# Products of weights and values in a differential attention: three passes of split operands in place of one native float32 matmul

## Chip, cores and metric

The kernel runs on 1 core of one Trainium2 chip. The metric is the device time of one execution in microseconds (us). The kernel before took 2629.19 us as the median of 3 runs (2627.92 to 2631.38).

## What is computed

One layer of a streaming-encoder trunk on 1024 positions of width 1024, all in float32. One input projection feeds three branches (an mLSTM, a differential attention, a retention); their outputs are gated, merged, projected, and a gated feed-forward follows. The change lies in the differential attention: 8 heads, each with two sets of scores (64 wide) and values 128 wide.

```python
def diff_attention(q, k, v, lam):
    ...
    for blk in range(S // Q_BLOCK):            # Q_BLOCK = 128, S = 1024
        q0 = blk * Q_BLOCK
        kend = q0 + Q_BLOCK
        ...
        s = jnp.einsum('bqhcd,bkhcd->bhcqk', qb, kb)
        ...
        s = jnp.where(allowed, s + bias[None, :, None], -jnp.inf)
        p = jax.nn.softmax(s, axis=-1)
        a = p[:, :, 0] - lam * p[:, :, 1]
        outs.append(jnp.einsum('bhqk,bkhe->bqhe', a, vb))
    ...
hd = (rmsnorm(hd, diff_subln[l]) * (1.0 - lam_init)).reshape(B, S, DIFF_W)
```

## The kernel before

Nearly every matmul of the kernel works on split operands: a float32 value is kept as a high part (a copy in the reduced type float32r) and a low part (the rest, also float32r). `split_sbuf` makes both, with a copy on ScalarE (L105) and a subtraction on VectorE (L106). `mm3` multiplies two split operands in three passes into one PSUM bank: high by high (L111), high by low (L112), low by high (L113). The projections, the merges of the branches, the output projection and the feed-forward are made of such passes with 512 moving columns.

The differential attention (`diff_core`) walks through 64 units, 8 heads by 8 query blocks of 128, the longest block first. A unit has up to 8 key blocks (qb + 1 of them). Its steps:

- `scores`: for both score sets, one or two PSUM buffers of scores from split q and k (L837), then the distance bias and the row maximum on VectorE (L839), then the exponential on ScalarE (L844).
- `weights`: the two exponentials are combined with the ratio of their sums (VectorE L850, L854, GpSimd L851, L853).
- `turn`: each 128x128 block of weights is transposed on TensorE (L864) into PSUM, in groups of up to four blocks, and each group is copied to SBUF (L866): the first group by ScalarE, the second by VectorE.
- `values`: one native float32 matmul for each key block (L874), with the transposed weights as the loaded operand and 128 columns of the values as the moving one. Then ScalarE takes the sum of squares (L214), GpSimd makes the factor (L220, L221), ScalarE applies it (L880).
- `finish`, one unit later: the result is transposed (L890), scaled (L891), and stored for every four units.

While unit n is turned, the scores of unit n + 2 and the weights of unit n + 1 are made. The q, k and v of the next head are loaded in the units with five and four key blocks (`diff_load`, `diff_load_v`, on the SP queue). Between the units' steps a generator hands out the merge products of the other two branches as filler for TensorE (`weave`, at a fixed rate); those left over run after the attention. The order of the instructions on each engine is made by the Tile scheduler from the program; each engine then works through its own list in that order.

Buffers: tiles of 4 KB a partition come from one pool of 32 (`big`), those of 2 KB from one of 14 (`half_tile`), and there are two sets of four PSUM banks: the value products and the merges take one, the scores and all transposes the other.

Of the kernel before, what the change touches and what calls it, by code (L numbers as in the profile page):

```python
# [9 lines left out]
F32R = mybir.dt.float32r  # L10
# [5 lines left out]
P = 128  # L16
D = 1024
S = 1024
NT = S // P
# [21 lines left out]
def trunk(ctx: ExitStack, tc: tile.TileContext, x, norm_gains, w_in, mlstm_conv, mlstm_gate_bias,  # L41
          diff_lambda, diff_subln, w_mlstm_out, w_diff_out, w_ret_out, w_out, w_ffn_in, w_ffn_out,
          c_ident, c_dist, c_tri, c_ret, c_retcol, c_reset, out):
    nc = tc.nc
# [11 lines left out]
    def nm(s):  # L56
        counter[0] += 1
        return f"{s}_{counter[0]}"

    def big(shape, dtype=F32, name="t"):  # L60
        return pool.tile(shape, dtype, tag="T", bufs=N_T, name=nm(name))

    def small(shape, tag, dtype=F32, bufs=2):
        return pool.tile(shape, dtype, tag=tag, bufs=bufs, name=nm(tag))

    def psum(dense=False):

        return psp.tile([P, HALF], F32, tag="d" if dense else "m", bufs=N_D if dense else 8 - N_D, name=nm("ps"))
# [20 lines left out]
    dv_dram = dram.tile([S, D], F32, name="dv_dram")  # L89
# [6 lines left out]
    def half_tile(shape=(P, HALF), dtype=F32):  # L96
        return pool.tile(list(shape), dtype, tag="s2k", bufs=N_H, name=nm("s2k"))
# [6 lines left out]
    def split_sbuf(hi, lo, src):  # L104
        nc.scalar.copy(hi, src)  # L105
        nc.vector.tensor_sub(lo, src, hi.bitcast(F32))  # L106

    def mm3(ps, lhs, rhs, start, stop, more=False):

        (lh, ll), (rh, rl) = lhs, rhs  # L110
        nc.tensor.matmul(ps, lh, rh, start=start, stop=False, skip_group_check=more)  # L111
        nc.tensor.matmul(ps, lh, rl, start=False, stop=False, skip_group_check=more)  # L112
        nc.tensor.matmul(ps, ll, rh, start=False, stop=stop, skip_group_check=more)  # L113
# [96 lines left out]
    def square_sum(src, n, tag, junk=None):  # L210
        if junk is None:
            junk = small([P, n], "junk", BF16 if n > HALF else F32, bufs=1)
        ss = small([P, 1], tag + "s", bufs=4)
        nc.scalar.activation(junk, src, AF.Square, accum_out=ss)  # L214
        return ss

    def factor(dst, ss, scale, extra):

        t = small([P, 1], "fv", bufs=4)
        nc.gpsimd.tensor_scalar(t, ss, scale, extra, op0=ALU.mult, op1=ALU.add)  # L220
        nc.gpsimd.tensor_tensor(dst, t, expo[:, 0:1], op=ALU.pow)  # L221
# [451 lines left out]
    def cols_at(t, a, b):  # L673
        return t[0][:, a:b], t[1][:, a:b]
# [133 lines left out]
            nc.sync.dma_start(d["q", sh][64 * i:64 * i + 64].bitcast(F32), q)  # L808

    def diff_load_v(hd, d):  # L810
        d["v"] = big([P, NT, P], name="dv")
        nc.sync.dma_start(d["v"], dv_dram[:, hd * P:(hd + 1) * P].rearrange("(t p) e -> p t e", p=P))

    diff_qk = [{} for _ in range(DH)]

    def half_cols(c):
        return slice((c % 4) * P, (c % 4 + 1) * P)

    def diff_core():
# [36 lines left out]
        def turn(u):  # L856
            qb = u["qb"]
            u["at"] = []
            for g in range((qb + 4) // 4):
                n = min(4, qb + 1 - g * 4)  # L860
                ps = psum()
                for i in range(n):
                    kb = g * 4 + i
                    nc.tensor.transpose(ps[:, i * P:(i + 1) * P], u["sb"][0][:, kb * P:(kb + 1) * P], ident)  # L864
                at = half_tile()
                (nc.scalar.copy if g == 0 else nc.vector.tensor_copy)(at[:, :n * P], ps[:, :n * P])  # L866
                u["at"].append(at)

        def values(u):
            hd, qb = u["hd"], u["qb"]  # L870
            v = diff_qk[hd]["v"]
            o_ps = psum(True)
            for kb in range(qb + 1):
                nc.tensor.matmul(o_ps[:, :P], u["at"][kb // 4][:, half_cols(kb)], v[:, kb, :],  # L874
                                 start=kb == 0, stop=kb == qb)
            ss = square_sum(o_ps[:, :P], P, "d")
            fac = small([P, 1], "dfac", bufs=4)
            factor(fac, ss, 1.0 / P, u["eps"])
            hn = u["hn"] = small([P, HD], "hk", bufs=2)
            nc.scalar.activation(hn[:, :P], o_ps[:, :P], AF.Copy, scale=fac)  # L880
# [20 lines left out]
        for n, u in enumerate(units):  # L901
            hd, qb = u["hd"], u["qb"]
# [446 lines left out]
    def head(dst, cols, kinds, hd):  # L1349
        for i, (c, evac) in enumerate(zip(cols, kinds)):  # L1350
            c += hd * HD
            yield of((c, c + P), evac(lambda j, i=i: dst[hd][:, 2 * i + j, :], hd))

    units = []
    for hd in range(MH):
        q, k, o, v = head(m_dram, (C_MQ, C_MK, C_MO, C_MV),
                          (lambda dst, hd: convolved(dst, 2 * hd), lambda dst, hd: convolved(dst, 8 + 2 * hd),
                           lambda dst, hd: stored(dst, AF.Sigmoid), lambda dst, hd: stored(dst)), hd)
# [88 lines left out]
    ps = psum()  # L1447
# [92 lines left out]
```

## Time and profile before

| what | value |
|---|---|
| median of 3 runs | 2629.19 us (2627.92 to 2631.38) |
| the profiled execution | 2628.78 us, of which 2627.0 us from the first to the last instruction (its span) |
| mean granted TensorE clock | 0.992 |
| TensorE (PE) busy | 2520.3 us, 96% of the span |
| VectorE (DVE), ScalarE (ACT), GpSimd (POOL) busy | 1650.2, 1245.9, 331.8 us |
| chain that ended last | 73% PE, 12% issue, 5% DVE, 4% ACT |
| the differential attention | from about 1347 to 1747 us of the span |

Times in rows are in us from the start of the span unless marked ns. A matmul's record is longer than its share of the engine, because matmuls are pipelined: what one costs is read from start to start. A row of the timeline gives start, length and, after the operation, how many instructions were merged in it (x14).

### The profile page before, as it was taken

What the parts mean: (1) busy time and instruction counts of PE and PEld (TensorE: products, weight loads), DVE (VectorE), ACT (ScalarE), POOL (GpSimd) and SP (SyncE); (2) the same over time, 40 slices, a digit from 0 to 9 for tenths busy, and PEclk for the clock granted to TensorE, in tenths of its full rate; (3) what the DMA queues carried; (4) which work ended last, traced back from release to release, by engine and by line L of the source; (5) the groups of instructions that cost most, each with busy time, mean ns of one, the idle gap of its engine ahead of it and who ended that gap; (6) DMA issues with size and microseconds to landing.
All of it is one profiled execution on the core that took longest, in us unless ns stands there. A gap on an engine that the chain in (4) does not pass through costs nothing.

```text
span 2627.0 us, 35171 instructions
## 1 busy us (share of the span) xinstructions
PE 2520.3 (96%) x12061; PEld 2058.6 (78%) x12061; DVE 1650.2 (63%) x3164; ACT 1245.9 (47%) x2562; POOL 331.8 (13%) x657
## 2 busy tenths in 40 slices
PE   6989999999999999999999988999989999999997
PEld 5868887888888888888878776778877888888885
DVE  7767777666656666555556665653468655656756
ACT  6554554444444444444446555542365333334444
POOL 0001111000000000000003223332121110110000
PEclk9999999999999999999999999999999999999999
DMA  4344345454445545444467566745443333327342
GB/s 127 95 125 137 115 132 153 136 150 123 127 139 161 169 145 150 137 134 121 138 193 178 140 184 157 189 157 188 144 137 112 101 104 97 105 97 288 113 143 78
DMA packets 402078, 368.93 MB, mean 140 GB/s; under 512 B 18957, under 2 KB 302046, under 8 KB 401898
## 3 DMA queue, kind: packets, MB, share of 16 engines
q1 hardware_dynamic: 399424, 364.45, 46.3%
q10 hardware_dynamic: 2474, 2.22, 0.3%
q8 instruction: 95, 1.56, 0.3%
q14 instruction: 85, 0.70, 0.1%
HBM read 249.92 MB, written 116.69 MB: 140 GB/s over the span
## 4 chain that ended last, share of the span: by engine, by line
PE 73%; issue 12%; DVE 5%; ACT 4%; POOL 3%; DMA 3%; SPq 1%; ACTq 0%; DVEq 0%; POOLq 0%
PE ps L112 22%; PE ps L113 22%; PE ps L111 22%; PE ps L874 2%; PE ps L837 1%; DMA s2k<-branch 1%; ACT sb L844 1%; POOL dfac L221 1%; PE ps L690 1%; PE ps L649 1%; POOL fv L220 1%; DVE sb L839 1%; POOL xr L208 1%; DMA ws<-in_w_in_dram 1%; DVE wl L106 0%
## 5 line engine op out<-in xcount | busy, mean ns | idle before, releaser
L105 ACT CAST wh<-ws 128x512 fp32r<-128x512 f32 (+1 forms) x622 | 385.1, 623 | 708.5 <-PE ps L112 514.1
L106 DVE TENSOR_TENSOR wl<-ws,wh 128x512 fp32r<-128x512 f32 (+1 forms) x622 | 449.8, 726 | 255.7 <-ACT wh L105 245.5
L315 DVE TENSOR_TENSOR ws<-ws,ws 128x512 f32<-128x512 f32 x234 | 160.8, 689 | 105.7 <-DMA ws<-in_w_in_dram 60.5
L111 PE MATMUL ps<-bh,wh 128*128 128x512 f32 x384 | 155.5, 405 | 1.6 <-ACT bh L105 1.6
L112 PE MATMUL ps<-bl,wh 128*128 128x512 f32 x384 | 152.5, 397 | 0.2 <-DVE bl L106 0.2
L113 PE MATMUL ps<-bh,wl 128*128 128x512 f32 x384 | 152.1, 396 | 0.0
L328 ACT COPY s2k<-ps 128x512 f32<-128x512 f32 x234 | 135.8, 581 | 11.2 <-PE ps L113 11.0
L111 PE MATMUL ps<-S2h,wh 128*128 128x512 f32 x312 | 125.7, 404 | 4.9 <-ACT s2k L328 4.9
L111 PE MATMUL ps<-A11h,wh 128*128 128x512 f32 x312 | 126.3, 405 | 2.7 <-ACT A11h L272 2.7
L112 PE MATMUL ps<-S1l,wh 128*128 128x512 f32 x312 | 123.5, 396 | 2.7 <-DVE S1l L106 2.7
L111 PE MATMUL ps<-S3h,wh 128*128 128x512 f32 x312 | 125.2, 401 | 0.9 <-ACT s2k L328 0.9
L111 PE MATMUL ps<-S1h,wh 128*128 128x512 f32 x312 | 124.2, 401 | 1.8 <-ACT S1h L105 1.7
L111 PE MATMUL ps<-A22h,wh 128*128 128x512 f32 x312 | 124.9, 400 | 0.8 <-DVE s2k L454 0.6
L112 PE MATMUL ps<-wl,wh 128*128 128x512 f32 x308 | 120.5, 392 | 4.8 <-DVE wl L106 4.8
L111 PE MATMUL ps<-S4h,wh 128*128 128x512 f32 x312 | 124.8, 400 | 0.0
L111 PE MATMUL ps<-A12h,wh 128*128 128x512 f32 x312 | 124.7, 400 | 0.0
L112 PE MATMUL ps<-S2l,wh 128*128 128x512 f32 x312 | 124.5, 400 | 0.0
L112 PE MATMUL ps<-A11l,wh 128*128 128x512 f32 x312 | 124.3, 398 | 0.1
L112 PE MATMUL ps<-A12l,wh 128*128 128x512 f32 x312 | 123.8, 397 | 0.5 <-DVE A12l L280 0.5
L113 PE MATMUL ps<-S2h,wl 128*128 128x512 f32 x312 | 124.1, 398 | 0.0
L113 PE MATMUL ps<-A11h,wl 128*128 128x512 f32 x312 | 124.0, 398 | 0.0
L113 PE MATMUL ps<-A12h,wl 128*128 128x512 f32 x312 | 123.9, 397 | 0.0
(301 smaller groups left out, 6434.1 us busy)
## 6 DMA issues: line engine op xcount, KB each, us to landing
ws<-in_w_in_dram SPq DMA_DIRECT2D x112, 512.0 KB, 4.5
ws<-in_w_ffn_in_dram SPq DMA_DIRECT2D x44, 512.0 KB, 4.3
m_dram<-s2k SPq DMA_DIRECT2D x64, 256.0 KB, 2.0
ch<-m_dram SPq DMA_DIRECT2D x32, 512.0 KB, 5.3
r_dram<-s2k SPq DMA_DIRECT2D x64, 256.0 KB, 2.3
ch<-r_dram SPq DMA_DIRECT2D x32, 512.0 KB, 4.7
qk_dram<-s2k SPq DMA_DIRECT2D x64, 256.0 KB, 2.7
dk<-qk_dram SPq DMA_DIRECT2D x64, 256.0 KB, 5.6
```

Of the source, the lines that this page charges most:

```text
L105: nc.scalar.copy(hi, src)
L106: nc.vector.tensor_sub(lo, src, hi.bitcast(F32))
L111: nc.tensor.matmul(ps, lh, rh, start=start, stop=False, skip_group_check=more)
L112: nc.tensor.matmul(ps, lh, rl, start=False, stop=False, skip_group_check=more)
L113: nc.tensor.matmul(ps, ll, rh, start=False, stop=stop, skip_group_check=more)
L208: nc.gpsimd.tensor_tensor(dst, t, expo[:, 0:1], op=ALU.pow)
L220: nc.gpsimd.tensor_scalar(t, ss, scale, extra, op0=ALU.mult, op1=ALU.add)
L221: nc.gpsimd.tensor_tensor(dst, t, expo[:, 0:1], op=ALU.pow)
L315: nc.vector.tensor_sub(*sub[r])
L328: nc.scalar.copy(t, ps)
L649: nc.tensor.transpose(ps[:, j * P:(j + 1) * P], ch[:, i + j, :], ident)
L874: nc.tensor.matmul(o_ps[:, :P], u["at"][kb // 4][:, half_cols(kb)], v[:, kb, :], start=kb == 0, stop=kb == qb)
```

## The change

The values of a head are loaded as before, and then split into a high and a low tile; the transposed weights are split out of PSUM instead of being copied; and each product of a weight block and a value block is `mm3`, three passes, in place of one native float32 matmul. After the change the lines behind L811 stand two further down (L866 transposes, L839 scores, L846 exponential, L882 scaling, L892 output transpose), and the value products have the lines L111 to L113, told from the others by their tiles (dvh and dvl).

```diff
     def diff_load_v(hd, d):
-        d["v"] = big([P, NT, P], name="dv")
-        nc.sync.dma_start(d["v"], dv_dram[:, hd * P:(hd + 1) * P].rearrange("(t p) e -> p t e", p=P))
+        raw = big([P, NT, P], name="dv")
+        nc.sync.dma_start(raw, dv_dram[:, hd * P:(hd + 1) * P].rearrange("(t p) e -> p t e", p=P))
+        d["v"] = big([P, NT, P], F32R, "dvh"), big([P, NT, P], F32R, "dvl")
+        split_sbuf(*d["v"], raw)
...
-                at = half_tile()
-                (nc.scalar.copy if g == 0 else nc.vector.tensor_copy)(at[:, :n * P], ps[:, :n * P])
+                at = half_tile([P, n * P], F32R), half_tile([P, n * P], F32R)
+                split_sbuf(*at, ps[:, :n * P])
                 u["at"].append(at)
...
             for kb in range(qb + 1):
-                nc.tensor.matmul(o_ps[:, :P], u["at"][kb // 4][:, half_cols(kb)], v[:, kb, :],
-                                 start=kb == 0, stop=kb == qb)
+                b = (kb % 4) * P
+                mm3(o_ps[:, :P], cols_at(u["at"][kb // 4], b, b + P), (v[0][:, kb, :], v[1][:, kb, :]), kb == 0, kb == qb)
```

On TensorE, the unit with three key blocks of the first head, before (dv is the value tile, s2k the copied weights, hk the output of the unit before; the brackets say which engines' semaphores a row waits for):

```order
L890 MATMUL ps_13513<-ident,hk_13466 128x128 [waits Activation_49]
L874 MATMUL ps_13516<-dv_12808,s2k_13486 128x128 [waits Activation_49]
L874 MATMUL ps_13516<-dv_12808,s2k_13486 128x128 x2
L864 MATMUL ps_13529<-ident,s2k_13432 128x128 [waits DVE_49,PE_49]
L864 MATMUL ps_13529<-ident,s2k_13432 128x128
```

The same unit after (s2k_13572 is the high half of the weights, s2k_13573 the low half; the two rows with bh, bl and wh are filler):

```order
L892 MATMUL ps_13601<-ident,hk_13552 128x128 [waits DVE_49,Activation_49]
L111 MATMUL ps_13604<-dvh_12810,s2k_13572 128x128 [waits Activation_49]
L112 MATMUL ps_13604<-dvl_12811,s2k_13572 128x128
L111 MATMUL ps_13664<-bh_12850,wh_13016 128x512
L112 MATMUL ps_13664<-bl_12851,wh_13016 128x512
L113 MATMUL ps_13604<-dvh_12810,s2k_13573 128x128 [waits DVE_49]
L111 MATMUL ps_13604<-dvh_12810,s2k_13572 128x128
L112 MATMUL ps_13604<-dvl_12811,s2k_13572 128x128
L113 MATMUL ps_13604<-dvh_12810,s2k_13573 128x128
L111 MATMUL ps_13604<-dvh_12810,s2k_13572 128x128
L112 MATMUL ps_13604<-dvl_12811,s2k_13572 128x128
L113 MATMUL ps_13604<-dvh_12810,s2k_13573 128x128
```

Three native products have become nine passes, and the third pass waits for VectorE where before only the copy on ScalarE was waited for.

On ScalarE, in the unit with four key blocks of the second head, before (junk is the sum of squares of that unit, hk its scaled output, the CASTs are filler's weights):

```order
L844 ACTIVATE s2k_14014,sm_14016<-s2k_14014,nmx_14028 128x256 [waits DVE_49]
L891 ACTIVATE s2k_13812<-ps_14031,sub_col 128x128 [waits PE_49]
L214 ACTIVATE junk_14040,ds_14041<-ps_14035 128x128 [waits PE_49,Activation_49]
L880 ACTIVATE hk_14047<-ps_14035,dfac_14043 128x128 [waits Pool_49]
L105 CAST wh_14232<-ws_13856 128x512 [waits PE_49]
```

The same place after (dvh is the high half of the third head's values):

```order
L846 ACTIVATE s2k_14192,sm_14194<-s2k_14192,nmx_14206 128x256 [waits DVE_49]
L105 CAST dvh_14172<-dv_14170 128x1024 [waits DMAHW6_49]
L214 ACTIVATE junk_14226,ds_14227<-ps_14213 128x128 [waits PE_49,Activation_49]
L882 ACTIVATE hk_14233<-ps_14213,dfac_14229 128x128 [waits Pool_49]
L105 CAST wh_14434<-ws_13998 128x512 [waits PE_49]
L105 CAST s2k_14254<-ps_14250 128x384 [waits PE_49]
```

The copy of the next head's values, which waits for its DMA, has come in ahead of the sum of squares and the scaling of the running unit.

## Rows read from the trace of the kernel before

**Rows 1.** The page: span, and busy time of TensorE and its weight loads.

```profile
span 2627.0 us, 35171 instructions
...
PE 2520.3 (96%) x12061; PEld 2058.6 (78%) x12061; DVE 1650.2 (63%) x3164; ACT 1245.9 (47%) x2562; POOL 331.8 (13%) x657
```

**Rows 2.** Table by stretch: stretch, its length, busy us (instructions) of each engine.

```profile
core 0: us, PE busy (x) PEld busy (x) DVE busy (x) ACT busy (x) POOL busy (x), PEclk, DMA share, GB/s
...
1306.00:1347.00 41.00, 41.00 (x177) 33.06 (x176) 17.56 (x28) 17.78 (x31) 0.00 (x0) 1.00 0.60 169
1347.00:1747.00 400.00, 360.20 (x2011) 297.04 (x2010) 241.96 (x761) 223.42 (x632) 121.78 (x266) 0.98 0.62 167
1747.00:1855.00 108.00, 106.61 (x459) 85.19 (x459) 45.71 (x69) 30.69 (x55) 28.07 (x21) 1.00 0.56 183
```

**Rows 3.** Waits of TensorE, 1347 to 1747: total us, times, longest.

```profile
PE ps L837 <- ACT s2k L866: 8.9, 13, 1.3
PE ps L890 <- ACT hk L880: 7.4, 10, 1.2
```

**Rows 4.** The value products' line L874: records, min/median/max ns, first and last start.

```profile
L874 PE MATMUL ps<-dv,s2k x576: 270/275/422, 1370.1 to 1746.9; 128*128 128x128 f32 x192
```

**Rows 5.** Timeline of TensorE: a run of native value records and what follows.

```profile
1509.56 1.73 PE L874 MATMUL ps<-dv,s2k 128*128 128x128 f32 x14
1511.04 0.48 PE L111 MATMUL ps<-bh,wh 128*128 128x512 f32 x1
```

**Rows 6.** Timeline of TensorE: four score passes of 128 columns and what follows.

```profile
1490.79 0.64 PE L837 MATMUL ps<-dk,dq 128*128 128x128 f32 x4
1491.26 0.30 PE L890 MATMUL ps<-ident,hk 128*128 128x128 f32 x1
```

**Rows 7.** Timeline: two such passes behind a 512-column one; then the second alone.

```profile
1422.20 0.33 PE L837 MATMUL ps<-dk,dq 128*128 128x128 f32 x2
...
1422.26 0.27 PE L837 MATMUL ps<-dk,dq 128*128 128x128 f32 x1
```

**Rows 8.** Timeline: passes of a three-pass product with 256 columns (retention).

```profile
1091.81 0.28 PE L111 MATMUL ps<-s2k,s2k 128*128 128x256 f32 x1
1091.93 0.28 PE L112 MATMUL ps<-s2k,s2k 128*128 128x256 f32 x1
1092.05 0.28 PE L113 MATMUL ps<-s2k,s2k 128*128 128x256 f32 x1
```

**Rows 9.** Groups by shape, 1347 to 1747: busy us, mean ns, idle before.

```profile
L866 ACT COPY s2k<-ps 128x512 f32<-128x512 f32 x40 | 23.2, 580 | 6.2 <-PE ps L864 6.1
L1017 DVE TENSOR_TENSOR s2k<-ps,s2k 128x512 f32<-128x512 f32 x29 | 19.9, 687 | 14.2 <-PE ps L113 13.6 <-DMA s2k<-gate 0.6
L844 ACT ACTIVATE sb<-sb,nmx 128x1024 f32<-128x1024 f32 x16 | 18.3, 1146 | 3.1 <-DVE nmx L843 3.1
L854 DVE SCALAR_TENSOR_TENSOR sb<-sb,rat,sb 128x1024 f32<-128x1024 f32 x8 | 10.3, 1282 | 2.1 <-POOL rat L851 2.1
```

**Rows 10.** The value load of head 2 on the SP queue; DMA issues by line (landing).

```profile
1440.27 0.38 SPq L812 DMA_DIRECT2D dv<-dv_dram  x1
...
dk<-qk_dram SPq DMA_DIRECT2D x64, 256.0 KB, 5.6
```

**Rows 11.** Timeline of ScalarE at that place: sum of squares, scaling.

```profile
1440.30 0.27 ACT L214 ACTIVATE junk<-ps 128x128 f32<-128x128 f32 x1
...
1441.74 0.37 ACT L880 ACTIVATE hk<-ps,dfac 128x128 f32<-128x128 f32 x1 [1.09 <-POOL dfac L221]
```

**Rows 12.** Timeline of TensorE: the transpose of that result.

```profile
1443.36 0.29 PE L890 MATMUL ps<-ident,hk 128*128 128x128 f32 x1
```

**Rows 13.** Timelines of the SP queue and ScalarE: the same at heads 4 and 6.

```profile
1532.07 0.54 SPq L812 DMA_DIRECT2D dv<-dv_dram  x1
...
1534.08 0.37 ACT L880 ACTIVATE hk<-ps,dfac 128x128 f32<-128x128 f32 x1 [1.09 <-POOL dfac L221]
...
1644.78 0.54 SPq L812 DMA_DIRECT2D dv<-dv_dram  x1
...
1645.54 0.37 ACT L880 ACTIVATE hk<-ps,dfac 128x128 f32<-128x128 f32 x1 [1.09 <-POOL dfac L221]
```

## The prediction

> **What bounds the kernel now.** I read the page first, then a table by stage, then the rows of the attention stage in order of time. TensorE (PE) is busy in 2520 of 2627.0 us [rows 1]: the kernel is a stream of matmuls, and a stage costs what its matmuls cost plus the holes in them. The change touches one stage. The differential attention runs from 1347 to 1747 us; there PE is busy 360.2 of 400 us, so some 40 us are holes, while VectorE (DVE) has 242 and ScalarE (ACT) 223 us of work [rows 2]. In the 41 us ahead of the stage PE is never idle, and in the 108 us behind it, where the merge products that were not used up as filler are run off, it is idle for 1.4 us [rows 2]. So PE time added to the stage comes back in the span unless it falls into one of the holes.
>
> The holes are short and scattered: the longest totals are scores that wait for ACT to empty a PSUM buffer (8.9 us in 13 pieces) and the transpose that waits for the normalised output (7.4 us in 10) [rows 3]. They are latencies of the chain PE, ACT, DVE, POOL, PE within one unit (one head, 128 queries), not a full engine.
>
> **The passes on PE.** 288 products of weights and values (36 for each of 8 heads) stand in the trace as 576 records [rows 4]: a native product leaves two records. A run of 14 of them goes from 1509.56 to 1511.04 us [rows 5], which is 0.106 us each and 0.211 us a product. The changed code issues three passes for each product, 864 in all, each with its own weight load and 128 moving columns. What does one such pass cost? The trace has the same form of instruction: scores of the first query block, split operands, 128x128 weights, 128 columns. Four in a row go from 1490.79 to 1491.26 [rows 6], 0.118 us each. That they aren't quicker is the point: 128 columns take no less than the load of the weights behind them. Below, the second of a pair behind a 512-column pass starts 0.06 us after the first [rows 7], the load having gone by behind the long pass; above, a three-pass product with 256 columns starts a pass every 0.12 us [rows 8]. So:
> - at 0.06 a product costs 0.18 and the change saves 288 x 0.031 = 9 us;
> - at the pace of the native records, 0.106, it costs 0.318, and adds 288 x 0.107 = 31 us;
> - at 0.12 it costs 0.36, and adds 43 us.
>
> I take 0.110, between the native records and the run of four, since in the new order the passes stand mostly in runs of three to twenty-four, and only the first two of a run can profit from a long pass ahead: 288 x (0.330 - 0.211) = **+34 us**.
>
> The rule that speaks for the change is in the Trainium skill, "FP8 and Floating Point Precision", section "TensorE Precision Notes": a true float32 product is four passes through the array. By it three passes would be three quarters of 0.211, and the sum would be 288 x 0.053 = 15 us to the good; the trace doesn't agree that passes are what is counted, for it has two records a product with 0.106 us each [rows 4, 5]. The skill's "TensorE: Matmul & The Clock Gate", section "LDWEIGHTS (loading the stationary operand)", has a load take columns / 1.2, which for 128 gives an estimate of 107 ns; the run of native records agrees.
>
> **The splits of the weights.** Per group of up to four transposed blocks, the old code has one copy out of PSUM: on ACT for the first group (0.580 us with 512 columns), on DVE for the second. The new code has a copy on ACT and then a subtraction on DVE, which reads the same PSUM buffer (0.687 us for such a subtraction with 512 columns) [rows 9]. As work this is cheap: ACT gains 32 copies of at most 0.580 (at most 19 us), DVE gains 96 subtractions of at most 0.687 and loses 32 copies (at most 66 less the 15 lost). Neither engine is full: 223 + 19 and 242 + 51 of 400 us. As latency it counts: the low half, and the PSUM buffer, are ready 0.580 + 0.687 = 1.27 us after the transposes where 0.58 did; of a second group later still, since both its steps queue behind those of the first. The third pass of the first product waits for it, and so do the scores that want the buffer. Nothing of that is paid if matmuls lie between: the order has four or more score passes there, of 0.23 us each where they have 512 columns, and mostly filler too. Bounds: 0, and 96 x 0.687 = 66 us with no cover at all. I take **+5 us**, near the lower end, because the order does put cover there.
>
> **The split of the values.** Once a head the 128x1024 value tile is copied on ACT and subtracted on DVE; the nearest rows of that width are 1.146 us on ACT and 1.282 on DVE [rows 9], 8 x 2.4 = 19 us of work off PE. What matters is where the ACT copy stands: for the values of heads 2, 4 and 6, which are loaded while the head before runs, it is ahead of the sum of squares or the scaling (L214, L882) of the unit with four key blocks, and it waits for its DMA. In the trace that DMA is issued at 1440.27, and a load of half its size on the same queue takes 5.6 us to land [rows 10]; an estimate from these two is that it's there at 1445.9. ACT did the sum of squares at 1440.30 and the scaling at 1441.74 [rows 11], PE the transpose of the result at 1443.36 [rows 12]. Behind the copy ACT would begin them at 1446.9 at best, and the transpose comes some 5 us later than it did. The same stands at heads 4 and 6: DMA at 1532.07 and 1644.78, the scaling at 1534.08 and 1645.54 [rows 13]. Three times 5 or 6 us less the filler that PE has there gives 0 to 18 us. I take **+9 us**. For the other heads the DMA is issued earlier, or the copy stands later.
>
> **What comes back.** With more matmuls in each unit some of the 40 us of holes close, because ACT and DVE get further meanwhile. Between 0 and 20; the values come at the end of a unit, ahead of the longest chain (sum of squares, POOL, scaling) and not inside it, so I take **-4 us**.
>
> **Sum.** 34 + 5 + 9 - 4 = +44 us. The profiled execution took 2628.8 us, 1.8 of them outside its span, and lies 0.4 us under the median of 2629.19: 2629 + 44 = **2673 us**, 1.7% slower. A measurement of this kernel tells about 0.2% (5 us) from no change.
>
> **The rivals.**
> 1. *The three passes are cheaper than the native two records.* If loads hide behind the pass ahead throughout, as in the pair at 0.06 us [rows 7], the passes save 9 us and the splits cost a little of it: some 2621 us, faster. It decides from a pass of less than 0.07 us (three times that equals 0.211). Against it stands that the run of four shows 0.118 with the same form [rows 6]. The rule of four passes would come out here too, at 2614 without the splits. Chance 0.05.
> 2. *The added passes fall into the holes.* 34 us of passes and 40 us of holes: if the units' latency sets the stage, PE's extra work is free and the time stays at 2629 to 2640. For it: holes in every stretch of the stage. Against: PE is busy for nine tenths of it, and the holes lie in front of scores and output transposes, which more value passes push back as well. Chance 0.07.
> 3. *The splits are the dear part.* If the low halves and buffers come late in most units (32 of the 66 us) and the value copies stop PE three times in full (18), the sum is 34 + 32 + 18 = 84 and the time 2713. For it: before, PE already waits for just these copies. Against: the order's cover. Chance 0.10.
>
> My forecast has 0.78.
>
> **How the numbers follow.** The forecast's own range is 31 to 43 us for the passes, 0 to 15 for the weights' splits, 0 to 18 for the values', -12 to 0 given back; not all at one end, that is +21 to +71, or 2650 to 2700. That leaves out rivals 1 and 2 and the upper one, about 0.2 together, so the range is 2650 to 2700. Faster: 0.05 from rival 1. Within 0.2%: 0.03, the better part of rival 2. Slower: 0.92.
>
> **What would show it.** PE's value rows: 864 records with the tiles of the split values, about 0.11 us from start to start in a run; with 0.06 the first step is wrong. The stage, 400 us now, is about 44 longer, and the stages ahead of and behind it don't change by more than 2 us. In the list of waits, PE waiting for the DVE subtraction of the weights: 5 us or less in all, or my second term is wrong. ACT idle before the value copy, for DMA: 15 us or so in all, and PE holes of up to 6 us at heads 2, 4 and 6. If PE's holes in the stage come to much less than 40 us, rival 2 had something; if to much more than 60, rival 3.

## The result, and the profile after

The changed kernel takes 2696.70 us as the median of 4 runs (2692.64 to 2701.08), against 2629.01 us for the kernel before; the ratio is 1.0262, with a 95% interval of [1.025, 1.0274]. That is slower by 2.6%, or 68.9 us of 2629.01 (the medians themselves lie 67.7 us apart). The profiled execution is one of the two quicker ones: 2692.72 us, 63.9 more than the profiled execution of before.

The page of the kernel after, its span and TensorE's busy time, against [rows 1]:

```profile
span 2690.9 us, 35861 instructions
...
PE 2573.1 (96%) x12349; PEld 2108.1 (78%) x12349; DVE 1693.2 (63%) x3236; ACT 1264.7 (47%) x2602; POOL 339.8 (13%) x657
```

The table by stretch of the kernel after, with the columns of [rows 2]:

```profile
1306.00:1347.00 41.00, 41.00 (x178) 32.65 (x177) 17.25 (x27) 17.62 (x30) 1.24 (x2) 1.00 0.60 164
1347.00:1810.00 463.00, 411.38 (x2311) 344.86 (x2310) 285.70 (x836) 243.96 (x677) 129.93 (x266) 0.95 0.54 146
1810.00:1920.00 110.00, 108.20 (x458) 86.81 (x458) 46.12 (x69) 30.59 (x55) 27.91 (x21) 0.98 0.55 179
```

The time is in the attention. The stretch ahead of it is as it was, the one behind has 1.8 us of holes where it had 1.4. The stage went from 400 to 463 us, and the row holds three things. PE is busy for 51 us more (360.2 to 411.4). Its holes grew from 40 to 52 us, where the passes might have closed some. And the granted clock fell from 0.98 to 0.95 of the stretch: at 0.95, 23 us of 463 are missing, at 0.98, 8 of 400.

The last point needs care, since an engine at half clock is busy for longer with the same work. From the first score pass to the last value record, the stage is 399.4 us before and 459.6 after (+60.2), of which 13.7 and 44.4 us have a granted clock of 0.50. A half-speed stretch loses half its length: 6.8 and 22.2 us, **+15**. Taken off PE's busy time (359.6 and 408.0), this leaves 352.8 and 385.8 us of work at full clock, **+33**. The holes are 39.8 and 51.6 us, **+12**. The rest of the 63.9 us is a stage that begins 2.7 us later and a tail that is 1.0 us longer. The clock is no accident of this one execution: its mean over the span is 0.982 to 0.985 in the four runs of after, and 0.988 to 0.994 in the runs of before that stand beside the experiments. The line between work and holes is less sharp. A record counts as busy to its modelled end, so each stop keeps a little of its idle time in the busy column; with the same passes and fewer stops, e1 below has +28 of work where after has +33.

The passes themselves, by the tile of the split values, and one run of them in the timeline of the kernel after (288 records each for L111, L112 and L113, 864 in all, against the 576 of [rows 4]):

```profile
L111 PE MATMUL ps<-dvh,s2k x288: 220/276/476, 1371.8 to 1809.6; 128*128 128x128 f32 x144
...
L113 PE MATMUL ps<-dvh,s2k x288: 220/275/476, 1376.1 to 1809.8; 128*128 128x128 f32 x144
```

```profile
1429.29 0.28 PE L111 MATMUL ps<-dvh,s2k 128*128 128x128 f32 x1
...
1431.18 0.28 PE L113 MATMUL ps<-dvh,s2k 128*128 128x128 f32 x1
1431.30 0.45 PE L111 MATMUL ps<-bh,wh 128*128 128x512 f32 x1
```

Eighteen passes stand from 1429.29 to the filler at 1431.30: 0.112 us each, 0.335 us a product, against 0.211 in [rows 5].

The waits of PE in the stage after (total us, times, longest), against [rows 3]:

```profile
PE ps L892 <- ACT hk L882: 18.6, 14, 3.7
PE ps L111 <- ACT s2k L105: 13.7, 18, 2.8
PE ps L839 <- DVE s2k L106: 9.3, 16, 2.1
...
PE ps L113 <- DVE s2k L106: 1.7, 6, 0.5
PE ps L892 <- DVE s2k L106: 1.3, 2, 1.0
```

Two more lines of the same view of the kernel before:

```profile
PE ps L874 <- ACT s2k L866: 2.3, 6, 0.8
...
PE ps L837 <- DVE s2k L866: 1.5, 4, 0.4
```

The output transpose waits for the scaling 18.6 us where it waited 7.4, and the first value pass waits for the copy of the weights 13.7 us where it waited 2.3. The wait of the scores for the buffer of the transposed weights has not grown: it is 9.3 us for the subtraction, and was 8.9 and 1.5 us for the copies. The groups by shape in the stage after (busy us, mean ns, idle before), against [rows 9]:

```profile
L106 DVE TENSOR_TENSOR s2k<-ps,s2k 128x512 fp32r<-128x512 f32 x48 | 32.4, 685 | 10.0 <-ACT s2k L105 8.2 <-DMA dk<-qk_dram 1.7
L105 ACT CAST s2k<-ps 128x512 fp32r<-128x512 f32 x48 | 27.3, 582 | 4.2 <-PE ps L866 4.1
...
L106 DVE TENSOR_TENSOR dvl<-dv,dvh 128x1024 fp32r<-128x1024 f32 x8 | 9.8, 1225 | 14.7 <-ACT dvh L105 14.7
...
L105 ACT CAST dvh<-dv 128x1024 fp32r<-128x1024 f32 x8 | 8.3, 1043 | 12.7 <-DMA dv<-dv_dram 12.7
```

The durations are near those of the rows taken before: 0.685 us and 0.582 for the weights, where 0.687 and 0.580 were taken; 1.225 and 1.043 for the values, 4 and 9% under the 1.282 and 1.146 taken. And ACT does wait for the values' DMA, 12.7 us in all, at six of the eight copies.

One of these copies stands in the unit with four key blocks of the fourth head. Its timeline on ScalarE (L846 exponentials, L214 sum of squares, L882 scaling) in the kernel after; the load was issued at 1563.66:

```profile
1566.90 0.19 ACT L846 ACTIVATION_READ_ACCUMULATOR s2k<-s2k,nmx 128x1 f32 x1
1568.50 1.05 ACT L105 CAST dvh<-dv 128x1024 fp32r<-128x1024 f32 x1 [1.41 <-DMA dv<-dv_dram]
1569.46 0.27 ACT L214 ACTIVATE junk<-ps 128x128 f32<-128x128 f32 x1
1569.62 0.19 ACT L214 ACTIVATION_READ_ACCUMULATOR junk<-ps 128x1 f32 x1
1571.60 0.37 ACT L882 ACTIVATE hk<-ps,dfac 128x128 f32<-128x128 f32 x1 [1.79 <-POOL dfac L221]
```

The same place on TensorE:

```profile
1572.03 0.33 PE L892 MATMUL ps<-ident,hk 128*128 128x128 f32 x1 [1.68 <-ACT hk L882]
1572.11 0.48 PE L111 MATMUL ps<-bh,wh 128*128 128x512 f32 x1
1572.43 0.40 PE L112 MATMUL ps<-bl,wh 128*128 128x512 f32 x1
1573.95 0.33 PE L111 MATMUL ps<-dvh,s2k 128*128 128x128 f32 x1 [1.12 <-ACT s2k L105]
...
1575.42 0.41 PE L112 MATMUL ps<-dvl,s2k 128*128 128x128 f32 x1
1575.63 0.41 PE L113 MATMUL ps<-dvh,s2k 128*128 128x128 f32 x1
```

And as two stretches, with the columns of [rows 2]:

```profile
1569.00:1574.00 5.00, 2.19 (x14) 1.47 (x12) 2.71 (x4) 3.21 (x9) 1.57 (x2) 1.00 0.77 223
1574.40:1577.80 3.40, 3.40 (x14) 2.75 (x14) 2.29 (x10) 2.00 (x10) 0.26 (x1) 0.50 0.81 242
```

The sum of squares stands behind the copy and starts when it ends, and all that follows is late: PE is busy for 2.19 of 5 us. Then comes a stretch at half clock, in which PE is never idle and a pass takes 0.21 us from start to start.

### The profile page after: what moved, and what is told of

It is laid out like the page before. It is cut to its first block, busy times and chain, and to the rows that moved or that the text cites. A ratio compares the mean times of both kernels' runs of the same rounds, so it can differ in the third digit from the quotient of the medians.

```text
span 2690.9 us, 35861 instructions
## 1 busy us (share of the span) xinstructions
PE 2573.1 (96%) x12349; PEld 2108.1 (78%) x12349; DVE 1693.2 (63%) x3236; ACT 1264.7 (47%) x2602; POOL 339.8 (13%) x657
## 4 chain that ended last, share of the span: by engine, by line
PE 70%; issue 12%; DVE 6%; DMA 4%; ACT 4%; POOL 3%; SPq 1%; ACTq 0%; DVEq 0%; POOLq 0%
PE ps L112 22%; PE ps L113 22%; PE ps L111 22%; DMA dv<-dv_dram 1%; PE ps L839 1%; POOL dfac L221 1%; ACT sb L846 1%; DVE sb L841 1%; PE ps L690 1%; DVE s2k L106 1%; DVE wl L106 1%; PE ps L649 1%; POOL fv L220 1%; DMA s2k<-branch 1%; DMA dq<-qk_dram 1%
## 5 line engine op out<-in xcount | busy, mean ns | idle before, releaser
L111 PE MATMUL ps<-bh,wh 128*128 128x512 f32 x384 | 157.3, 410 | 0.0
L112 PE MATMUL ps<-bl,wh 128*128 128x512 f32 x384 | 155.3, 404 | 0.2 <-DVE bl L106 0.2
L113 PE MATMUL ps<-bh,wl 128*128 128x512 f32 x384 | 155.0, 404 | 0.0
L111 PE MATMUL ps<-S2h,wh 128*128 128x512 f32 x312 | 125.6, 404 | 4.9 <-ACT s2k L328 4.9
L111 PE MATMUL ps<-A11h,wh 128*128 128x512 f32 x312 | 126.0, 405 | 2.3 <-ACT A11h L272 2.3
L112 PE MATMUL ps<-S1l,wh 128*128 128x512 f32 x312 | 124.7, 400 | 2.5 <-DVE S1l L106 2.5
L111 PE MATMUL ps<-S1h,wh 128*128 128x512 f32 x312 | 124.9, 403 | 2.0 <-ACT S1h L105 2.0
L111 PE MATMUL ps<-S3h,wh 128*128 128x512 f32 x312 | 125.2, 401 | 0.9 <-ACT s2k L328 0.9
L111 PE MATMUL ps<-A22h,wh 128*128 128x512 f32 x312 | 124.8, 400 | 0.9 <-DVE s2k L454 0.9
L112 PE MATMUL ps<-wl,wh 128*128 128x512 f32 x308 | 120.5, 392 | 5.4 <-DVE wl L106 5.4
L111 PE MATMUL ps<-S4h,wh 128*128 128x512 f32 x312 | 125.2, 401 | 0.0
L111 PE MATMUL ps<-A12h,wh 128*128 128x512 f32 x312 | 124.7, 400 | 0.0
L113 PE MATMUL ps<-S1h,wl 128*128 128x512 f32 x312 | 124.4, 399 | 0.0
L112 PE MATMUL ps<-S2l,wh 128*128 128x512 f32 x312 | 124.2, 399 | 0.0
L112 PE MATMUL ps<-A11l,wh 128*128 128x512 f32 x312 | 124.0, 398 | 0.1
L113 PE MATMUL ps<-S2h,wl 128*128 128x512 f32 x312 | 124.0, 398 | 0.0
L112 PE MATMUL ps<-S4l,wh 128*128 128x512 f32 x312 | 123.9, 397 | 0.0
L112 PE MATMUL ps<-A12l,wh 128*128 128x512 f32 x312 | 123.5, 396 | 0.4 <-DVE A12l L280 0.4
```

## The experiments

Each was timed beside the kernel before on one chip. Some leave out or repeat part of the computation; so their times stand for the work that they do. The cuts of code show the lines that matter; what else an edit changes is told in words. The table puts them together. The stage is from the first score pass to the last value record; PE and DVE busy are from the table by stretch over it, the holes are the rest, and "half" is the time with a granted clock of 0.50. In every one of these stages stand the same 696 passes of filler, so the stages can be compared. They are from one execution each, though, and among the runs of one kernel the mean granted clock varies by 0.001 to 0.006, where 0.003 is some 8 us of the span: a few us more or less at half clock are not a difference between two kernels. And the scheduler makes the order on the engines anew for each kernel, so that two of them differ by more than the lines shown.

| kernel | ratio to before, 95% interval | stage | PE busy | holes | half | DVE busy |
|---|---|---|---|---|---|---|
| before | 1 | 399.4 | 359.6 | 39.8 | 13.7 | 241.5 |
| after | 1.0262 [1.025, 1.0274] | 459.6 | 408.0 | 51.6 | 44.4 | 282.9 |
| e1: three passes, no splits | 1.0105 [1.0086, 1.0125] | 420.6 | 395.7 | 24.9 | 30.7 | 243.6 |
| e2: both splits, native product | 1.012 [1.0105, 1.0135] | 429.3 | 375.8 | 53.5 | 41.0 | 281.0 |
| e3: one pass, no splits | 0.9991 [0.9979, 1.0003] | 391.6 | 336.0 | 55.6 | 27.3 | 240.8 |
| e4: as after, values split later | 1.0188 [1.0172, 1.0204] | 442.4 | 402.4 | 40.0 | 34.1 | 281.5 |
| f1: values' split alone | 1.0015 [1.0006, 1.0025] | 403.2 | 361.9 | 41.3 | 17.1 | 248.4 |
| f2: weights' split alone | 1.0062 [1.0045, 1.0079] | 411.7 | 367.6 | 44.1 | 20.5 | 269.8 |
| f3: as e4, second copy on VectorE | 1.0216 [1.0195, 1.0237] | 449.4 | 410.9 | 38.5 | 47.8 | 295.7 |
| f4: as e4, two wider passes | 1.0172 [1.0157, 1.0187] | 440.0 | 376.7 | 63.3 | 30.7 | 297.3 |
| g1: three passes and weights' split | 1.021 [1.0193, 1.0227] | 451.4 | 409.3 | 42.1 | 44.4 | 273.5 |
| g2: as after, values loaded earlier | 1.0262 [1.0246, 1.0277] | 463.2 | 413.1 | 50.1 | 54.6 | 282.5 |
| g3: copies of weights all on ScalarE | 0.999 [0.9981, 0.9999] | 394.3 | 357.4 | 36.9 | 10.2 | 231.8 |
| h1: one more subtraction, from SBUF | 1.0086 [1.007, 1.0103] | 419.6 | 366.7 | 52.9 | 17.1 | 288.1 |

**e1: the passes alone.** Weights and values are written once in the reduced type (lines not shown), and each product is three passes over the same operands.

```diff
-                nc.tensor.matmul(o_ps[:, :P], u["at"][kb // 4][:, half_cols(kb)], v[:, kb, :],
-                                 start=kb == 0, stop=kb == qb)
+                a = u["at"][kb // 4][:, half_cols(kb)]
+                for i in range(3):
+                    nc.tensor.matmul(o_ps[:, :P], a, v[:, kb, :], start=kb == 0 and i == 0, stop=kb == qb and i == 2)
```

> Three float32r passes of 128 columns for each product, but no splits: the transposed weights are copied once into a float32r tile, by the engines of before, and the values are loaded straight into one; both low halves are left out, so all three passes multiply the same pair. My theory, passes at 0.11 us in place of 0.211 us a product: +34 us of TensorE time, some 2629 + 34 = 2663, and up to 2670 if the clock falls a little more often. If instead the passes are hidden in the holes and the splits are the dear part, within 10 us of 2629. If the passes alone bring the whole change, near 2697.

Measured: 2655.34 us, +27.6 by the ratio. A run of passes in its timeline, and what follows it:

```profile
1426.85 2.77 PE L876 MATMUL ps<-dv,s2k 128*128 128x128 f32 x23
1429.45 0.45 PE L111 MATMUL ps<-bh,wh 128*128 128x512 f32 x1
```

That is 2.60 us for 23 passes, 0.113 each: the price is the pass's own and has nothing to do with splits. PE is busy for 36 us more, the holes are 15 us smaller, and half clock loses 8.5 us more, which is part of the busy time; at full clock the work is 28 us more. Passes alone do fall into holes in part; in the changed kernel the holes are 12 us larger than before.

**e2: the splits alone.** Both splits are made as in the changed kernel (lines not shown), and the native product takes the high halves.

```diff
+                b = (kb % 4) * P
-                nc.tensor.matmul(o_ps[:, :P], u["at"][kb // 4][:, half_cols(kb)], v[:, kb, :],
+                nc.tensor.matmul(o_ps[:, :P], u["at"][kb // 4][0][:, b:b + P].bitcast(F32), v[0][:, kb, :].bitcast(F32),
                                  start=kb == 0, stop=kb == qb)
```

> Both splits as in the changed kernel, but one native float32 product of the two high halves in place of three passes; the low halves are made and read by nobody, so their part of the product is left out. My theory, the other half of the loss of 68 us: the splits hold PSUM buffers and the scaling chain longer, 20 to 34 us, so 2649 to 2663, with the half-speed clock on in more than the 14 us of the attention stage that it had before. If the splits only cost together with the passes, 2629 to 2640.

Measured: 2661.78 us, +31.5. Operations off TensorE, on two engines that are not full, cost as much as the passes do (the two intervals overlap). The holes are 14 us larger, and half clock loses 14 us more.

**e3: one pass, no splits.** As e1 with `range(1)`: two passes of each product are left out.

> As the run with three passes without splits, but one pass for each product (high by high alone, both low halves left out). By the price of a pass of 0.11 us TensorE is spared 288 x (0.211 - 0.11) = 29 us, 2600 if all of it comes back. If the units' latency sets the stage, the spared time turns into holes and half-speed clock, and it ends at 2615 to 2629. The step from one pass to three should be 576 x 0.11 = 63 us if TensorE is the bound throughout.

Measured: 2627.46 us, the time of before within the interval. PE is busy for 24 us less, and its holes are 16 us larger. The stage is 8 us shorter and begins 1.4 us earlier, but the time of all runs is the same. So the stage has a floor near the time of before that PE's work does not set; that it is the latency of the units is the reading that fits, not one that this run shows.

**e4: the values split later.** The changed kernel, with the split of the next head's values at the last unit of the running head. On ScalarE the copy then stands in the unit with two key blocks, at one head in that with one; in the changed kernel it is the one with four at four of the seven heads, and that with two or three at the others.

```diff
+                if qb == 0:
+                    diff_split_v(diff_qk[hd + 1])
             turn(u)
```

> The changed kernel, complete, with the split of the next head's values written three units later (at the last unit of the head, when the load has long landed). My theory of the values' split: 9 us of the loss, and the waits of ScalarE for that DMA (12.7 us in the changed kernel) are gone: 2685 to 2690. If those waits were covered by filler anyway, 2697; if the copy of 1.04 us itself is in the way wherever it stands, 2697 too, but then without a DMA wait in the list.

Measured: 2681.02 us, 1.0188 against the 1.0262 of after: 19 us come back (16 between the medians). ACT's wait for that DMA is 0.3 us, the holes are 40.0 us, and half clock loses 5 us less.

**f1: the values' split alone,** with native products and weights copied as before (the edits of `diff_load_v`, without the others).

> The values are split where the changed kernel splits them; the transposed weights are copied as before, and one native product multiplies them by the high half of the values (the low half is left out). The late split gave back some 16 us of the change, so by my theory the early split costs 14 to 19 us by itself: 2643 to 2648, with waits of ScalarE for the load of the values and of TensorE for the scaled output. If it only costs together with the passes, under 2635.

Measured: 2631.79 us, +4, less than was expected. The scheduler had put the copies mostly one or two units later here than in the changed kernel, and ACT waits for the DMA 1.4 us. So this run doesn't price the place that the copy has in the changed kernel.

**f2: the weights' split alone,** with native products of the high half.

```diff
-                at = half_tile()
-                (nc.scalar.copy if g == 0 else nc.vector.tensor_copy)(at[:, :n * P], ps[:, :n * P])
+                at = half_tile([P, n * P], F32R), half_tile([P, n * P], F32R)
+                split_sbuf(*at, ps[:, :n * P])
```

> The transposed weights are split as in the changed kernel; the values are as before, and one native product multiplies the high half of the weights by them (the low half is left out). Both splits together cost 32 us, so by additivity this costs 13 to 18 us: 2642 to 2647, with TensorE waiting for the copy on ScalarE ahead of the values (8 us of such waits before). If the buffer that VectorE holds longer is the price, the waits stand ahead of the scores instead; if the value split is the whole loss, 2630.

Measured: 2644.48 us, +16 (1.0062).

**g1: passes and weights' split,** the values written once in the reduced type. It is the changed kernel without the values' split.

> Three passes and the split of the weights, but no split of the values: they are loaded straight into one float32r tile, which stands for both halves in the passes. Passes alone cost 27 us and the split of the weights alone 16; if they add up, 2628 + 43 = 2671. If the split's latency comes to lie beside the longer passes, 2660; if the two make each other worse, above 2680, and then the values' split would be a small part of the change.

Measured: 2685.80 us, +55 (1.021). The two parts alone cost 27.6 and 16, together 44; so 11 us more are paid where they meet. The holes say where: e1 closes 15 us of them, g1 none (42.1 against 39.8). The first value pass waits for the copy of its weights 14.4 us here, and 2.6 in e1 (first the line of g1, then that of e1):

```profile
PE ps L111 <- ACT s2k L105: 14.4, 16, 3.4
```

```profile
PE ps L876 <- ACT s2k L866: 2.6, 5, 1.8
```

The values' split in its place is then the rest of the 68.9, some 14 us.

**g2: the values loaded earlier.** The changed kernel, with the load issued two units sooner; from the second head on that is 16.8 us or more ahead of the copy.

```diff
+                if qb == 5:
+                    diff_load_v(hd + 1, diff_qk[hd + 1])
                 if qb == 4:
...
-                    diff_load_v(hd + 1, diff_qk[hd + 1])
+                    diff_split_v(diff_qk[hd + 1])
```

> The changed kernel, complete; only the load of the next head's values is issued ahead of the other loads of that head, so that it has landed when ScalarE comes to the copy; the copy itself stands near its old place, ahead of the scaling. If the wait for the load is the price of the values' split, about what the late split gave: 2680 to 2686, and the waits of ScalarE for that load are under 2 us (12.7 in the changed kernel). If the copy's place is the price, 2692 to 2697.

Measured: 2699.53 us, ratio 1.0262, that of after. No wait for the values' DMA is left, and nothing has come back. But the scheduler put the copy earlier too, into the unit with five key blocks at six of the seven heads, so the run doesn't price the wait by itself; what it shows is that a copy that waits for nothing can cost as much. Its timeline on ScalarE there (L895 scales the transposed output, L884 is the scaling):

```profile
1564.74 0.35 ACT L895 ACTIVATE s2k<-ps,sub_col 128x128 f32<-128x128 f32 x1
1564.99 1.03 ACT L105 CAST dvh<-dv 128x1024 fp32r<-128x1024 f32 x1
1565.93 0.27 ACT L214 ACTIVATE junk<-ps 128x128 f32<-128x128 f32 x1
1566.10 0.19 ACT L214 ACTIVATION_READ_ACCUMULATOR junk<-ps 128x1 f32 x1
1566.19 0.58 ACT L105 CAST s2k<-ps 128x512 fp32r<-128x512 f32 x1
```

And on TensorE:

```profile
1566.82 0.33 PE L111 MATMUL ps<-dvh,s2k 128*128 128x128 f32 x1 [1.36 <-ACT s2k L105]
1566.98 0.27 PE L112 MATMUL ps<-dvl,s2k 128*128 128x128 f32 x1
1568.50 0.33 PE L894 MATMUL ps<-ident,hk 128*128 128x128 f32 x1 [1.25 <-ACT hk L884]
```

The same two matmuls of the same unit in the kernel after, where the copy is not in this unit:

```profile
1564.27 0.33 PE L111 MATMUL ps<-dvh,s2k 128*128 128x128 f32 x1 [0.40 <-ACT s2k L105]
...
1565.38 0.33 PE L892 MATMUL ps<-ident,hk 128*128 128x128 f32 x1 [0.68 <-ACT hk L882]
```

A copy that waits for nothing still delays the sum of squares and the copy of the weights by its 0.94 us, and PE waits 2.61 us there instead of 1.08. Summed over the second to the eighth head, from one scaled output to the next, PE's holes in the units with five key blocks are 16.7 us in g2 and 9.1 or 9.2 in after, e4 and g1; in those with four they are 0.8 in g2, 10.2 in after, 0.4 in e4 and g1. The holes go where the copy goes. The rest of what g2 loses against e4 is half clock, 54.6 us against the 34.1 of e4.

**f3: the second group's copy back on VectorE,** with e4's place for the values.

```diff
-                split_sbuf(*at, ps[:, :n * P])
+                (nc.scalar.copy if g == 0 else nc.vector.tensor_copy)(at[0], ps[:, :n * P])
+                nc.vector.tensor_sub(at[1], ps[:, :n * P], at[0].bitcast(F32))
```

> The changed kernel with the late value split, complete; the high half of the second group is copied by VectorE, as the kernel before did it, so ScalarE has 32 copies less in the stage. If the copies queued on ScalarE are what the first passes wait for (13.8 us ahead of L111 in the late-split kernel), 5 to 10 us less than with the late split alone: 2671 to 2676. If VectorE's longer list is what counts, the same 2681 or up to 8 more.

Measured: 2682.31 us, 1.0216 [1.0195, 1.0237]: no better than e4. The first of its expectations fell; the other, that VectorE's longer list counts, fits it (VectorE is busy 14 us more than in e4). PE still waits 14.4 us for the copies of the weights.

**f4: two wider passes.** High and low halves of the values lie side by side, so that the high weights take 256 columns in one pass and the low weights 128; the two halves of the result are then added. With e4's place.

```diff
+                nc.tensor.matmul(o_ps[:, :2 * P], ah, w.rearrange("p a e -> p (a e)"), start=kb == 0, stop=False)
+                nc.tensor.matmul(o_ps[:, :P], al, w[:, 0, :], start=False, stop=kb == qb)
+            o_sb = small([P, P], "osb", bufs=2)
+            nc.scalar.copy(o_sb, o_ps[:, P:2 * P])
+            nc.vector.tensor_add(o_sb, o_ps[:, :P], o_sb)
```

> Late value split, complete, and two passes in place of three: the high half of the weights with high and low values side by side (256 columns), the low half with the high values (128 columns), the two halves of the result added by one ScalarE copy and one VectorE addition per unit. Passes by the rows: 0.12 + 0.11 = 0.23 us a product in place of 0.33, 29 us less TensorE time than with three passes: 2652 if all of it comes back. The longer chain behind the values (copy and addition, some 0.6 us, 64 times) gives back part: 2655 to 2670. If the holes set the stage, 2675 or more.

Measured: 2673.58 us, 1.0172 [1.0157, 1.0187]. Two products in its timeline on TensorE (L883 the wide pass, L884 the narrow one):

```profile
1428.64 0.33 PE L883 MATMUL ps<-dvv,s2k 128*128 128x256 f32 x1
1428.81 0.22 PE L884 MATMUL ps<-dvv,s2k 128*128 128x128 f32 x1
1428.87 0.33 PE L883 MATMUL ps<-dvv,s2k 128*128 128x256 f32 x1
1429.03 0.22 PE L884 MATMUL ps<-dvv,s2k 128*128 128x128 f32 x1
```

A product now takes 0.23 us, close to the native 0.211, and PE is busy for 26 us less than in e4. The stage gets 2 us shorter. PE's waits say why:

```profile
PE ps L883 <- ACT s2k L105: 27.0, 23, 5.1
PE ps L902 <- ACT hk L892: 18.3, 32, 1.5
```

The holes are 63.3 us: the added copy and sum lengthen the chain of each unit, and the first product still waits for the weights' copy.

**g3: all copies of the weights on ScalarE,** no subtraction, native products.

```diff
-                at = half_tile()
-                (nc.scalar.copy if g == 0 else nc.vector.tensor_copy)(at[:, :n * P], ps[:, :n * P])
+                at = (half_tile([P, n * P], F32R),)
+                nc.scalar.copy(at[0], ps[:, :n * P])
```

> The kernel with the split of the weights alone (native product of the high half), without the subtraction: only the copies of the second groups have moved from VectorE to ScalarE, and no low half is made. If the subtraction on VectorE, and the PSUM buffer that it holds, is what that split costs (16 us), 2628 to 2634. If the copies queued one behind the other on ScalarE are, 2638 to 2645.

Measured: 2628.26 us, 0.999 [0.9981, 0.9999]. ScalarE's added copies cost nothing; f2's 16 us come with the subtraction, which is what f2 has besides, with a second buffer of 2 KB for each group.

**h1: the subtraction, reading SBUF.** The kernel before, with a VectorE subtraction for each group that reads the copy and other SBUF data.

```diff
                 u["at"].append(at)
+                nc.vector.tensor_sub(half_tile([P, n * P], F32R), at[:, :n * P], u["sb"][0][:, g * HALF:g * HALF + n * P])
```

> The kernel before with one more VectorE subtraction for each group of transposed weights, 96 in all; it reads the copy in SBUF and other SBUF data, not the PSUM buffer, and its output is used by nothing. So VectorE's list is as long as with the weights' split, but PSUM buffers come free as before. If VectorE's longer list is the price of the split, the time is that of f2_weight_split_only, 2640 to 2647 us. If it is the PSUM buffer that the subtraction holds, 2628 to 2634 us.

Measured: 2650.14 us, 1.0086 [1.007, 1.0103], +22.6. PE, ScalarE and GpSimd never wait for this subtraction (one DMA issue does, for 3.1 us), and it holds no PSUM buffer; yet it costs no less than f2's. Its largest group, and that of f2:

```profile
L868 DVE TENSOR_TENSOR s2k<-s2k,sb 128x512 fp32r<-128x512 f32 x40 | 29.1, 728 | 5.6 <-ACT s2k L866 5.6
```

```profile
L106 DVE TENSOR_TENSOR s2k<-ps,s2k 128x512 fp32r<-128x512 f32 x48 | 32.4, 685 | 6.0 <-ACT s2k L105 6.0
```

VectorE is busy 9.6 us less than before in g3, 28.3 more in f2 and 46.6 more in h1, and the times differ by -2.6, +16 and +22.6. The time goes with the length of VectorE's list, at about half of it in f2 and h1, though VectorE is busy for no more than 0.69 of h1's stage. That a held buffer adds nothing at all is not shown by this, only that it isn't needed to explain f2. Nor is the scheduler's new order told from the list: the sequence of scores, transposes, value products and filler on PE differs from that of before in some 100 places in h1, as in f2, and in 44 in g3, which costs nothing.

## Why the prediction was right, and where its sum was not

Direction, range and the forecast's reason held: the passes are slower than the native product and the work isn't hidden. The range held by 3 us, and by luck in part: its width was made for the four terms of the sum, and what used it up was not among them. The number was 24 us below the median, and by the trace of after the sum missed it in the main in one place: it had no term for the clock. The work at full clock is +33 (forecast: 34), the holes +12 (forecast: 5 + 9 - 4 = 10), the clock +15 (forecast: nothing); the rest is the stage's later start (2.7 us, where I had allowed 2; ahead of the stage 17.1 us are at half clock, 6.8 before), the tail, and 4 us that the median run lies above the profiled one. The experiments show besides that the +10 was right by terms that erred against each other.

**The passes, +34: right in the price of a pass, less sure in the sum.** 0.112 us each where 0.110 was taken. But e1, with the same passes and no splits, adds 28 us to the work at full clock and 27.6 us to the time, under the 31 to 43 that I had allowed; some 5 of the 33 us in after come with the splits. What spoke for the rival of cheap passes is real, but for other shapes: in f4 a 128-column pass behind a 256-column one takes 0.06 us, and the 256-column one 0.17; in runs of 128-column passes it is 0.11 throughout.

The Trainium skill's rule of four passes for a true float32 product ("FP8 and Floating Point Precision", section "TensorE Precision Notes") would have three passes at three quarters of 0.211 us. They take 0.335, and the measurement decides.

**The weights' splits, +5: mis-sized.** They are 16 us alone (f2) and 27 on top of the passes (g1 against e1). The step that failed is "near the lower end, because the order does put cover there". For the third pass the cover holds: L113 waits 1.7 us. PE's waits that name the subtraction come to 12.3 us (9.3, 1.7, 1.3), where the test that I had set was 5; but most of them are scores that want the buffer, and these waited 10.4 us for the copies before. What grew is the wait of the first value pass for the copy ahead of the subtraction, from 2.3 to 13.7 us, and that of the output transpose, and the test didn't ask for these. And h1 shows that a subtraction costs as much when no matmul waits for it or for a PSUM buffer that it holds. I had asked only who reads it and who wants its buffer; that it delays what is behind it on VectorE is the reading that fits, with the scheduler's order as the rival that is left.

**The values' split, +9 (0 to 18): in its bounds by g1 (11 us between the medians, 14 by the ratios), at or just above their end by e4 (16 and 19), with a mechanism that holds in part.** The copy waits for its DMA in a sum near the forecast (12.7 us; I said 15 or so), but in six places of 1.3 to 3.2 us and not in three of 5, so that the sum came out is luck in part. The unit with four key blocks does stop behind it. Yet the wait isn't needed for the price: g2 takes it away, with the copy a unit earlier, and the time stays. What costs by g2's rows is the copy's place ahead of the sum of squares and of the next copy of the weights; e4, which takes away both the wait and the place, frees the 19 us. It is no constant of the split: e2 against f2 makes it 15 us with the copies mostly one or two units later than in after, f1 only 4 in such places. Why these two differ is open.

**What comes back, -4: too small, and then spent.** The passes alone close 15 us of holes (e1), which is more than I allowed, and in g1, with the weights' split, nothing of it is left. The parts were priced one by one and share one slack.

**The clock, not in the sum.** Half clock costs 22 us of the stage after and 7 before. The trace of before had four such stretches in the stage; one, from 1546.0 us, follows 6 us in which PE is busy for 3.23. I didn't ask whether the change would make more such places. After, the stop behind a value copy is followed by one (2.19 of 5 us, then 0.50). That the stops cause the falls is argued from their order, not shown by a run.

Of the rivals, the dear splits were nearer than their chance: by e1, g1 and after, passes are 28 us and splits 41 of the 68.9; in the other order, by e2 and after, the splits are 31.5 and the passes 37. The parts don't add up, so neither share is the true one. That passes fall into holes is half true of e1. None of the versions tried beats the kernel before by as much as 0.2%.

## What to carry to other kernels

Where a native float32 product has only 128 moving columns, count its records and their pace from start to start before it is replaced: here three passes of 0.112 us stand against two records of 0.106. When an operation is added to an engine with spare time, ask what stands behind it in that engine's list, not only who reads its output or wants its buffers. And where PE is nearly full but waits in many short pieces, price the parts together, for they hide in the same holes, and look at the granted clock of the stretches that follow the places where PE will stop.

## What was unexpected of the hardware

The time at half clock in the stage ran from 10.2 us (g3) to 54.6 (g2) and doesn't follow the sum of holes: e1 has 24.9 us of holes and 30.7 at half clock, f4 63.3 and 30.7, f2 44.1 and 20.5. Ahead of every fall PE was partly idle. The 14 stages have 90 falls, and in the 5 us ahead of a fall PE was idle for 2.1 us on the median, where the stages have 0.3 to 0.7 us in 5 on the mean; in the fall shown it was 2.81 us, and in e1 1.17 us ahead of 6.8 us at 0.50 from 1579.3. What decides it was not tried. And taking work off TensorE, busy for 96% of the span, was worth next to nothing: 24 us less busy in e3 than before and 26 less in f4 than in e4, where each unit's chain also grew, moved the time by 2 and 4 us.
